# A two-layer decoder trunk: order of the out-projection's rows, lags of the norm feeds, and order of the key copies

## The chip, the cores and the metric

One core of one Trainium2 chip. The metric is device time in microseconds (us) of one execution; lower is better. Engines are named as the profile names them: PE (TensorE matmul) and PEld (its weight load), DVE (VectorE), ACT (ScalarE), POOL (GpSimd), SP (SyncE, which issues most DMAs here). L12 is line 12 of the kernel.

## The reference

x is 256 tokens by 1024. Two layers, each with a half-step SwiGLU FFN, a mixer, and a second half-step FFN:

```python
for layer in range(DEPTH):
    if layer == N_A_LAYERS:
        k_pads, v_pads = _shared_kv(x, kv_norm, w_kv, k_gain)
    x = x + 0.5 * _swiglu(_rms(x, norm_gain[layer, 0]), ffn_w_in[layer, 0], ffn_w_out[layer, 0])
    h = _rms(x, norm_gain[layer, 1])
    if layer < N_A_LAYERS:
        x = x + _hgrn2(h, a_w_in[layer], ...)
    else:
        x = x + _dilated_attention(h, b_w_q[j], b_q_gain[j], b_w_o[j], k_pads, v_pads, rel_bias)
    x = x + 0.5 * _swiglu(_rms(x, norm_gain[layer, 2]), ffn_w_in[layer, 1], ffn_w_out[layer, 1])
```

`_swiglu(h, w_in, w_out)` is `(silu(gate) * up) @ w_out` with `gate, up = split(h @ w_in)` and an inner width of 2816. The first mixer is a gated linear recurrence (8 heads), the second an attention with 16 heads of 64 in three groups of windows and dilations (128, 1), (512, 4), (2048, 16), with RMS-normed queries and keys and a shared bias by distance. Both mixers end with an out-projection of 1024 by 1024.

## The kernel before

**Precision by halves.** Every float32 operand of a large product is split into two fp32r numbers, high and low: ScalarE makes the high one by a copy or a scaled copy, VectorE subtracts it from the source to get the low one. Each product is then three matmuls: high by high, high by low, low by high. For weights this is `load_part` (L233 ff.): one or two DMAs on SP into one of 4 `raw` buffers, the ACT cast `wh` (L241), the DVE subtraction `wl` (L242), six buffers each. A part is two weight rows (two blocks of 128 in the contracted dimension) by 512 columns.

**Two kinds of product.** `products` (L248 ff.) takes tokens as the stationary side: for each of two token tiles `t`, three matmuls of 512 columns per weight row (L256, L257, L258), and after the last row a `consume(t, ...)`. `linear_T` (L271 ff.) takes weights as the stationary side: per pair of accumulators and part a "turn" of four pairs of matmuls (L312 with 512 columns: both halves of all 256 tokens at once; L308 with 256). In the first use of a norm its turns are sorted so that the first four need only rows 0 to 3 of the input, that is the left half of x, and turns five to eight the right half.

**The norm is applied late.** x itself, times the gain, is fed to the product; the factor 1/rms per token is applied to the result. `Norm.feed(n, t)` (L360 ff.) does this for the column half `n` (0 left, 1 right) and token tile `t` of x: four PE transposes into a PSUM bank (L365), four ACT scaled copies (L217) and four DVE operations (L220). A norm can have several operand sets with different gains: the norm ahead of layer 1's first FFN has two, `xT` for the FFN and `xK` for the keys and values of the attention. Then `square` (L375 ff.) sums squares on ACT (L380); after the fourth of these `finish` makes the scale by two DVE operations and a POOL power (L393), and `spread` (L398 ff.) transposes the scale on PE (L402) into a row by token that ACT copies out (L408). The products' consumers that need the row wait in a list until it is there.

**Ticks.** The order of the program is written by hand with a list of deferred jobs. `products` calls `tick()` after each token tile (six matmuls with a part of two rows, three with one row), `linear_T` after each turn. `defer(lag, fn)` runs `fn` in the lag-th tick from then; a job that was deferred just ahead of a tick with lag 1 runs in that very tick. A scheduler in the compiler then sets the final order on each engine; an engine runs its own queue in order.

**Lags the change touches.** `FEED_LAG = 1` between an add into x and the feed of that piece (L439); `ROW_LAG = 2` between `finish` and `spread` (L396); `NORM_LAG = 6` between the scaling of normed queries or keys and their transposes (L969).

**Adds and feeds.** `add_to_x` (L431 ff.) adds a finished accumulator into x on DVE (L435 after an out-projection, L437 after an FFN) and defers the feed of the next norm. In the FFN's second product the left half of the columns is finished 132 matmuls ahead of the right half's end.

**Out-projection** (L445 ff.). Both halves' accumulators are open together. Parts of two rows: left 0-5, then right 0-5, then both last parts are loaded and their rows run by turns, in order left 6, right 6, left 7, right 7. So when the left half is done, one row of the right half (six matmuls) is left.

**Attention.** The keys and values are made in four quarters of four heads each (`Quarter`, L1016 ff.). For three quarters the blocks are: all keys of two groups; the third's keys and the first's values; the other values. The last quarter has its own: first block keys of all three groups for the first pair of heads and the keys of group 0 for the second pair; second block the rest of the keys and some values; then the scores of the first pair; then the last values. `normed` (L952 ff.) squares, sums and scales keys, then transposes them on PE (`tpn`, L974), and `put_keys` (L1062 ff.) copies them out: for group 0 with halves, as each head has to stand in both halves of the partitions, high in its own and low, and the other way; for each of two heads ACT copies the high part (L1070), DVE makes the low one (L1071), ACT copies both to the other half (L1072 from PSUM, L1073 from SBUF). The other groups take one ACT copy (L1065). `scores` (L1126 ff.) reads them (L1136, L1137, L1143), `transposed` transposes the probabilities (`tpp`, L1189) and ACT copies them out (L1190). All transposes, scores and small products share the four PSUM banks of `psm`.

## Time and profile before

| | us |
|---|---|
| median of 3 runs | 1183.0 (1181.94 to 1184.51) |
| profiled execution | 1182.2, its span 1180.4 |
| PE busy | 1163.2 |
| PEld busy | 971.5 |
| DVE busy | 775.5 |
| ACT busy | 706.7 |
| POOL busy | 223.0 |

The profile is of one execution. Busy time is the union of an engine's instructions; a matmul's end is modelled, and matmuls overlap in the pipeline. In a timeline a line has the start in us from the span's start, the duration, the engine, the line, the operation, what it writes and reads, the shape and the count; the idle time of the engine just before it and what ended that time stand in square brackets.

### The profile page before, as it was taken

The page shows a single profiled execution, that of the slowest core. Times are in us where ns is not written, and L with a number is a line of the kernel's source. Part 1 is how long each engine was busy: PE and PEld are TensorE (multiplying, and loading weights), DVE is VectorE, ACT ScalarE, POOL GpSimd, SP SyncE. Part 2 cuts the span into 40 slices and gives each one's busy share as a digit, 9 for nine tenths or more (in the row PEclk, how much of TensorE's full clock was granted, in tenths as well). Part 3 has the DMA queues.
Part 4 walks back from the last instruction along what each step waited for, and adds up shares of the span by engine and source line. Part 5 has one row for each costly group of instructions (what it writes and reads, how often), then busy time and mean ns, then how long its engine had stood idle before and what let it go on. Part 6 is the DMA issues. An engine that isn't in the chain of part 4 may idle for free.

```text
span 1180.4 us, 18859 instructions
## 1 busy us (share of the span) xinstructions
PE 1163.2 (99%) x6774; PEld 971.5 (82%) x6774; DVE 775.5 (66%) x1263; ACT 706.7 (60%) x1283; POOL 223.0 (19%) x240
## 2 busy tenths in 40 slices
PE   9999999999999999999999999999999999999998
PEld 6888888888878888878888887888877777888886
DVE  6666655898766676666666556866776766666652
ACT  6656544876556565556556446657668686665541
POOL 2232201310012322003322002221210200323200
PEclk9999999999999999999999999999999999999999
DMA  8565666554545665555665665565465544556571
GB/s 273 159 207 176 208 201 182 177 160 163 163 150 168 196 189 203 181 179 167 188 197 173 223 192 181 174 195 176 139 182 149 153 130 130 168 175 203 185 234 44
DMA packets 181713, 209.28 MB, mean 177 GB/s; under 512 B 15483, under 2 KB 139843, under 8 KB 181620
## 3 DMA queue, kind: packets, MB, share of 16 engines
q1 hardware_dynamic: 180928, 207.68, 56.4%
q8 instruction: 53, 0.87, 0.3%
q10 hardware_dynamic: 692, 0.40, 0.1%
q14 instruction: 40, 0.33, 0.1%
HBM read 205.89 MB, written 1.10 MB: 175 GB/s over the span
## 4 chain that ended last, share of the span: by engine, by line
PE 83%; DVE 7%; issue 6%; ACT 2%; POOL 1%; DMA 1%; ACTq 0%; SPq 0%; DVEq 0%; POOLq 0%
PE acc L312 28%; PE acc L308 14%; PE acc L256 13%; PE acc L258 13%; PE acc L257 13%; DVE wl L242 2%; DMA raw<-in_ffn_w_in_dram 1%; PE tpn L974 1%; PE ob L1214 1%; PE tpp L1189 1%; POOL rs L428 1%; ACT wh L241 0%; PE tp L365 0%; DVE xT L220 0%; DVE kd L709 0%
## 5 line engine op out<-in xcount | busy, mean ns | idle before, releaser
L242 DVE TENSOR_TENSOR wl<-raw,wh 128x1024 fp32r<-128x1024 f32 x384 | 482.9, 1280 | 163.3 <-ACT wh L241 161.8
L241 ACT CAST wh<-raw 128x1024 fp32r<-128x1024 f32 x384 | 394.7, 1051 | 179.2 <-PE acc L258 151.4
L312 PE MATMUL acc<-xT,wh 128*128 128x512 f32 x1184 | 409.1, 398 | 0.8 <-DVE u L328 0.8
L308 PE MATMUL acc<-xT,wl 128*128 128x256 f32 x1184 | 308.1, 281 | 0.0
L312 PEld LDWEIGHTS acc<-xT,wh 128*128 128x128 f32 x1184 | 212.3, 188 | 42.2 <-DVE u L328 1.1
L308 PEld LDWEIGHTS acc<-xT,wl 128*128 128x128 f32 x1184 | 223.6, 189 | 12.9
L258 PE MATMUL acc<-wh,hid 128*128 128x512 f32 x352 | 137.8, 391 | 0.0
L256 PE MATMUL acc<-wh,hid 128*128 128x512 f32 x352 | 137.8, 391 | 0.0
L257 PE MATMUL acc<-wl,hid 128*128 128x512 f32 x352 | 137.5, 391 | 0.0
L209 DVE TENSOR_TENSOR hid<-u,hid 128x256 fp32r<-128x256 f32 x88 | 37.5, 426 | 133.7 <-ACT hid L208 133.7
L477 POOL TENSOR_TENSOR g<-g,row 128x256 f32<-128x256 f32 x88 | 65.6, 746 | 294.3 <-DVE g L328 282.8
L312 PE MATMUL acc<-xK,wh 128*128 128x512 f32 x352 | 119.7, 395 | 0.0
L478 ACT ACTIVATE g<-g 128x256 f32<-128x256 f32 x88 | 36.8, 419 | 97.1 <-POOL g L477 97.1
L479 POOL TENSOR_TENSOR u<-u,g 128x256 f32<-128x256 f32 x88 | 84.6, 961 | 50.8 <-ACT g L478 48.9
L256 PE MATMUL acc<-wh,xK 128*128 128x512 f32 x224 | 92.8, 414 | 0.0
L428 POOL TENSOR_TENSOR rs<-var,mhalf 128x8 f32<-128x8 f32 (+1 forms) x32 | 49.3, 1542 | 226.5 <-DVE var L426 226.5
L308 PE MATMUL acc<-xK,wl 128*128 128x256 f32 x352 | 90.5, 277 | 0.0
L208 ACT CAST hid<-u 128x256 fp32r<-128x256 f32 x88 | 35.7, 406 | 90.9 <-POOL u L479 90.9
L258 PE MATMUL acc<-wh,xK 128*128 128x512 f32 x224 | 88.7, 396 | 0.4 <-DVE xK L209 0.4
L257 PE MATMUL acc<-wl,xK 128*128 128x512 f32 x224 | 88.2, 394 | 0.0
L256 PE MATMUL acc<-wh,xT 128*128 128x512 f32 x192 | 78.0, 406 | 0.0
L258 PEld LDWEIGHTS acc<-wh,hid 128*128 128x128 f32 x352 | 66.0, 188 | 14.3
(176 smaller groups left out, 1472.0 us busy)
## 6 DMA issues: line engine op xcount, KB each, us to landing
raw<-in_ffn_w_in_dram SPq DMA_DIRECT2D x352, 256.0 KB, 4.2
raw<-in_ffn_w_out_dram SPq DMA_DIRECT2D x88, 512.0 KB, 4.6
raw<-in_w_kv_dram SPq DMA_DIRECT2D x72, 256.0 KB, 4.2
raw<-in_a_w_in_dram SPq DMA_DIRECT2D x32, 512.0 KB, 4.0
raw<-in_b_w_q_dram SPq DMA_DIRECT2D x24, 512.0 KB, 3.8
raw<-in_w_kv_dram SPq DMA_DIRECT2D x48, 128.0 KB, 2.4
raw<-in_a_w_out_dram SPq DMA_DIRECT2D x8, 512.0 KB, 3.5
raw<-in_b_w_o_dram SPq DMA_DIRECT2D x8, 512.0 KB, 3.7
```

Source lines behind the costliest of these rows:

```text
L209: nc.vector.tensor_tensor(l, src, h.bitcast(F32), op=ALU.subtract)
L241: casts.append(nc.scalar.copy(wh[:, :nk, :], raw[:, :nk, :]))
L242: nc.vector.tensor_tensor(wl[:, :nk, :], raw[:, :nk, :], wh[:, :nk, :].bitcast(F32), op=ALU.subtract)
L256: nc.tensor.matmul(ps[t], xs.h[:, kk, tok], wh[:, at, :], start=kk == 0, stop=False)
L257: nc.tensor.matmul(ps[t], xs.h[:, kk, tok], wl[:, at, :], start=False, stop=False)
L258: nc.tensor.matmul(ps[t], xs.l[:, kk, tok], wh[:, at, :], start=False, stop=kk == nkt - 1)
L308: nc.tensor.matmul(acc[:, 0:S], wl[:, k, w], xs.h[:, kk, :], start=False, stop=False)
L312: nc.tensor.matmul(acc, wh[:, k, w], xs.hl[:, kk, :, :].rearrange("p a t -> p (a t)"), start=kk == 0, stop=kk == KD - 1,)
L428: nc.gpsimd.tensor_tensor(r[:, :n], v[:, :n], mhalf[:, :n], op=ALU.pow)
L477: nc.gpsimd.tensor_tensor(g, g, norm.by_token, op=ALU.mult)
L478: nc.scalar.activation(g, g, AF.Silu)
L479: nc.gpsimd.tensor_tensor(u, u, g, op=ALU.mult)
```

## The change

1. `ROW_LAG` goes from 2 to 3.
2. `FEED_LAG` is now by half: 1 for the left, 2 for the right, after out-projections and FFNs alike. The right half's second feed thus runs in the tick after the last product's, which is the first tick of what follows.
3. In `feed` only the first operand set is put at once; the others follow three ticks later (`SECOND_LAG`), behind the square. Only the norm with `xT` and `xK` has a second set.
4. The out-projection's rows: left 0-5, right 0-3, then single rows left 6, right 4, right 5, left 7, right 6, right 7. When the left half is done, two rows of the right half (twelve matmuls) are left. A part is loaded where its first row is needed.
5. The transposes of the last quarter's keys come three ticks after their scaling (`LAST_LAG`), not six; the second pair's group 0 keys of its first block are put two ticks after the first's (`PAIR_LAG`).
6. `put_keys` for group 0: ACT copies the high parts of both heads from PSUM, then DVE makes both low parts, then ACT copies the high parts to the other half from SBUF (before: from PSUM), and DVE copies the low parts there (before: ACT). The queries' put gets the same order by engine: two ACT operations, then two DVE operations.

```diff
--- before.py
+++ after.py
@@ -40,24 +40,27 @@
 BIAS_LEN = (512, 128, 128)
 BT = 768
 SCW = S + P
-ROW_LAG = 2
+ROW_LAG = 3
 LB_LAG = 20
 SC_BUFS = 4
 WARM = 8
 WARM_ON = 10
-FEED_LAG = 1
+FEED_LAG = (1, 2)
+SECOND_LAG = 3
 GATE_LAG = 3
 SQUARE_LAG = 1
 MOVE_LAG = 6
 SQ0 = 4
 SQ_STEP = 1
 NORM_LAG = 6
+LAST_LAG = 3
 SCALE_LAG = 3
 LEVEL_LAG = 5
 UNIT_LAG0 = 3
 UNIT_LAG = 2
 SCORE_LAG = 5
 VALUE_LAG = 2
+PAIR_LAG = 2
 BLK = 32
 QUADS = (2, 8)
 DIAG_LAG = 5
@@ -363,14 +366,20 @@
             for c in range(4):
                 at = (4 * n + c) * P
                 nc.tensor.transpose(tp[:, c * P : (c + 1) * P], self.x[:, t, at : at + P], ident)
-            for g, halves in self.sets:
+
+            def put(g, halves):
                 halves.put_scaled(
                     4 * n,
                     slice(t * P, (t + 1) * P),
                     tp.rearrange("p (c t) -> p c t", c=4),
                     g[:, 4 * n : 4 * n + 4],
                 )
+
+            put(*self.sets[0])
             defer(SQUARE_LAG, lambda: self.square(n, t))
+            for g, halves in self.sets[1:]:
+
+                defer(SECOND_LAG, lambda g=g, halves=halves: put(g, halves))
 
         def square(self, n, t):
             if self.fed == 0:
@@ -436,7 +445,7 @@
         else:
             nc.vector.scalar_tensor_tensor(to, ps, scale, to, op0=ALU.mult, op1=ALU.add)
         if norm is not None:
-            defer(FEED_LAG, lambda: norm.feed(n, t))
+            defer(FEED_LAG[n], lambda: norm.feed(n, t))
         return to
 
     def half_of(w, n):
@@ -452,13 +461,17 @@
         def done(n):
             return lambda t, acc: add_to_x(x, n, t, acc, norm)
 
+        parts = {}
+
+        row_by_row = [(0, KD - 2), (1, KD - 4), (1, KD - 3), (0, KD - 1), (1, KD - 2), (1, KD - 1)]
         for n in range(2):
-            for k in range(0, KD - NK, NK):
+            for k in range(0, min(kk for nn, kk in row_by_row if nn == n), NK):
                 products(xs, ps[n], k, NK, KD, *part(n, k), done(n))
-        last = [part(n, KD - NK) for n in range(2)]
-        for k in range(NK):
-            for n in range(2):
-                products(xs, ps[n], KD - NK + k, 1, KD, *last[n], done(n), off=k)
+        for n, k in row_by_row:
+            k0 = k // NK * NK
+            if (n, k0) not in parts:
+                parts[n, k0] = part(n, k0)
+            products(xs, ps[n], k, 1, KD, *parts[n, k0], done(n), off=k - k0)
 
 
     def ffn(x, layer, f, norm, following, part_first=None):
@@ -949,7 +962,7 @@
 
             return slice(64 * c, 64 * c + 64), slice(64 - 64 * c, 128 - 64 * c)
 
-        def normed(ps, nh, mean, then):
+        def normed(ps, nh, mean, then, lag=NORM_LAG):
 
             sq = tmp4.tile([P, 512], F32, tag="s5", name="sqh")
             nc.scalar.activation(sq[:, : nh * HD], ps, AF.Square)
@@ -966,7 +979,7 @@
                     rs[:, :nh].unsqueeze(2).broadcast_to([P, nh, HD]),
                     op=ALU.mult,
                 )
-                defer(NORM_LAG, transposed)
+                defer(lag, transposed)
 
             def transposed():
                 tp = bank("tpn")
@@ -989,13 +1002,16 @@
                             qT[:, g - 1, 4 * a : 4 * a + 4, tok], reverse(tp), AF.Copy, scale=qkT[:, g : g + 1]
                         )
                         return
+                    ways = []
                     for c in range(2):
                         own, other = places(c)
                         to = q0[:, 8 * a + c : 8 * a + 8 : 2, tok]
-                        src, gain = reverse(tp)[own], qkT[own, 0:1]
-                        nc.scalar.activation(to[own], src, AF.Copy, scale=gain)
+                        ways.append((to[own], to[other], reverse(tp)[own], qkT[own, 0:1]))
+                    for high, low, src, gain in ways:
+                        nc.scalar.activation(high, src, AF.Copy, scale=gain)
+                    for high, low, src, gain in ways:
                         nc.vector.scalar_tensor_tensor(
-                            to[other], src, gain, to[own].bitcast(F32), op0=ALU.mult, op1=ALU.subtract
+                            low, src, gain, high.bitcast(F32), op0=ALU.mult, op1=ALU.subtract
                         )
 
                 normed(ps, 8, norm.eps(t), put)
@@ -1045,11 +1061,16 @@
                         c += n
 
                     def put(tp):
-                        for g, p0, p1, c0 in keys:
-                            self.put_keys(t, g, p0, p1, tp[:, c0 : c0 + p1 - p0, :])
+                        for i, (g, p0, p1, c0) in enumerate(keys):
+                            args = (t, g, p0, p1, tp[:, c0 : c0 + p1 - p0, :])
+                            if i > 0 and g == 0:
+
+                                defer(PAIR_LAG, lambda args=args: self.put_keys(*args))
+                            else:
+                                self.put_keys(*args)
 
                     if keys:
-                        normed(ps[:, : nk * P], 2 * nk, norm2.eps(t), put)
+                        normed(ps[:, : nk * P], 2 * nk, norm2.eps(t), put, NORM_LAG if self.j < 3 else LAST_LAG)
 
                 cols = []
                 for kind, g0, g1, p0, p1 in pieces:
@@ -1064,13 +1085,19 @@
                 if g > 0:
                     nc.scalar.copy(self.kT[:, g - 1, p0:p1, tok], tp)
                     return
+
+                ways = []
                 for c in range(2):
-                    own, other = places(c)
                     h, l = (v[:, 2 * p0 + c : 2 * p1 : 2, tok] for v in (self.kh, self.kl))
+                    ways.append((*places(c), h, l))
+                for own, other, h, l in ways:
                     nc.scalar.copy(h[own], tp[own])
+                for own, other, h, l in ways:
                     nc.vector.tensor_tensor(l[own], tp[own], h[own].bitcast(F32), op=ALU.subtract)
-                    nc.scalar.copy(h[other], tp[own])
-                    nc.scalar.copy(l[other], l[own].bitcast(F32))
+                for own, other, h, l in ways:
+                    nc.scalar.copy(h[other], h[own].bitcast(F32))
+                for own, other, h, l in ways:
+                    nc.vector.tensor_copy(l[other], l[own].bitcast(F32))
 
             def put_values(self, t, g, c0, c1, ps):
                 r = norm2.rstd(t)
```

## The prediction

> **What bounds the kernel now.** I read the page first: its first part and the chain that ended last.
>
> ```profile
> PE 1163.2 (99%) x6774; PEld 971.5 (82%) x6774; DVE 775.5 (66%) x1263; ACT 706.7 (60%) x1283; POOL 223.0 (19%) x240
> ...
> PE 83%; DVE 7%; issue 6%; ACT 2%; POOL 1%; DMA 1%; ACTq 0%; SPq 0%; DVEq 0%; POOLq 0%
> ```
>
> TensorE is busy for 99% and carries 83% of the chain, and the change takes no matmul and no transpose away. So it can only win where PE stands still, 1180.4 - 1163.2 = 17.2 us in all. The table of waits, for PE alone, says for whom it stands still:
>
> ```profile
> PE tp L365 <- DVE res L435: 3.3, 2, 1.7
> PE rp L402 <- POOL rstd L393: 2.4, 3, 1.4
> PE sp L1136 <- ACT kh L1072: 1.7, 1, 1.7
> ```
>
> Columns: total us, times, longest. These three are the largest, and each is a place that the change touches: the feeds after the out-projections, the transposes of the row scales, the keys. I then read the timeline engine by engine around each.
>
> **Left half earlier, right feed later (out-projection).** PE, then VectorE, at the end of the first out-projection; the last line is PE at the second:
>
> ```profile
> 334.01 0.66 PE L365 MATMUL tp<-ident,res 128*128 128x128 f32 x4 [1.65 <-DVE res L435]
> ```
> ```profile
> 329.33 1.37 DVE L435 TENSOR_TENSOR res<-acc,res 128x512 f32<-128x512 f32 x2 [1.09 <-PE acc L258]
> 331.09 1.23 DVE L242 TENSOR_TENSOR wl<-raw,wh 128x1024 fp32r<-128x1024 f32 x1 [0.39 <-ACT wh L241]
> 332.24 1.12 DVE L220 SCALAR_TENSOR_TENSOR xT<-tp,gT,xT 128x128 fp32r<-128x128 f32 x4
> 333.27 0.68 DVE L435 TENSOR_TENSOR res<-acc,res 128x512 f32<-128x512 f32 x1
> 333.87 1.12 DVE L220 SCALAR_TENSOR_TENSOR xT<-tp,gT,xT 128x128 fp32r<-128x128 f32 x4
> ```
> ```profile
> 991.13 0.65 PE L365 MATMUL tp<-ident,res 128*128 128x128 f32 x4 [1.67 <-DVE res L435]
> ```
>
> PE's last product is done at 334.01 - 1.65 = 332.36. The wait is put down to the third add (333.27), but the FFN's first matmul could not start then either: it reads both token halves of the first weight row, so it needs the first of the four pieces of the second L220 group, 333.87 + 1.12/4 = 334.15. That whole chain starts with the adds of the left half at 329.33. At present the left half ends 9 matmuls before the end (3 of its own second token tile, 6 of the last row of the right half); in the new order 15 (two rows of the right half). Matmul starts stand 0.23 apart:
>
> ```profile
> 928.50 0.39 PE L257 MATMUL acc<-wl,xK 128*128 128x512 f32 x1
> 928.72 0.39 PE L258 MATMUL acc<-wh,xK 128*128 128x512 f32 x1
> 928.95 0.49 PE L1189 MATMUL tpp<-ident,sc 128*128 128x128 f32 x3
> ```
>
> 6 x 0.23 = 1.38 earlier, so the first FFN matmul can start at 334.15 - 1.38 = 332.77 against 332.36: 0.41 of the 1.65 stays, 1.24 goes. Upper end: all 1.65. Lower end: the last row of the FFN's first chunk gets its weight buffer later in the new order (released 18 matmuls before the end instead of 24), so one more 1.23 us subtraction of L242 can fall between the adds and the feeds; then 1.38 - 1.23 = 0.15 is left. I take 1.24, as in the row order that is there. Two out-projections: **2.5 us**. The right feed's own step, one tick later, is costed at nothing: its eight transposes per boundary are the same work, and the FFN's first turn (made from the left half only) covers it. What is late next is turn five, which needs the right half; see the last rival. Nothing moves on the DMA queue but the order in which two weight parts of the out-projection are asked for: same eight loads, same bytes, four buffers ahead.
>
> **Scale transposes later.** PE at the three places where it waits for them (first and second out-projection, then the FFN with two operands):
>
> ```profile
> 340.64 0.43 PE L402 MATMUL rp<-ident,rstd 128*128 128x128 f32 x2 [0.51 <-POOL rstd L393]
> ```
> ```profile
> 997.76 0.43 PE L402 MATMUL rp<-ident,rstd 128*128 128x128 f32 x2 [0.49 <-POOL rstd L393]
> ```
> ```profile
> 530.28 0.43 PE L402 MATMUL rp<-ident,rstd 128*128 128x128 f32 x2 [1.44 <-POOL rstd L393]
> ```
>
> The right feed's extra tick and the row lag's extra tick put these two turns later, behind five turns instead of three. A turn is four pairs of matmuls, and a pair takes 0.35:
>
> ```profile
> 341.26 0.40 PE L312 MATMUL acc<-xT,wh 128*128 128x512 f32 x1
> 341.50 0.28 PE L308 MATMUL acc<-xT,wl 128*128 128x256 f32 x1
> 341.61 0.39 PE L312 MATMUL acc<-xT,wh 128*128 128x512 f32 x1
> ```
>
> After the first out-projection the FFN's pairs run from 334.4 (the transposes at 334.01 issued) to 340.13; less 0.6 for four more transposes that is 14 pairs, and at five turns, 20 pairs, they come 6 x 0.35 = 2.1 later, more than the 0.5 missing: **1.0 us** gained for both. At the third place the FFN starts at
>
> ```profile
> 520.63 0.39 PE L312 MATMUL acc<-xT,wh 128*128 128x512 f32 x1
> ```
>
> and PE stops at 528.84: 8.2 less 1.3 for eight transposes is some 20 pairs, five turns already. The queue there did not follow the text, and the lag alone gives nothing. There the second operands are the lever. ScalarE, then GpSimd:
>
> ```profile
> 524.46 1.18 ACT L217 ACTIVATE xK<-tp,gT 128x128 fp32r<-128x128 f32 x4
> 525.46 0.71 ACT L380 ACTIVATE junk<-res 128x512 f32<-128x512 f32 x1
> ```
> ```profile
> 528.60 1.63 POOL L393 TENSOR_TENSOR rstd<-tot,mhalf 128x2 f32<-128x2 f32 x1 [64.18 <-DVE tot L389]
> ```
>
> The last square (525.46) stands behind one xK group of 1.18, and VectorE has two such groups ahead of the scale. With both three ticks later the square starts about 1.0 earlier and VectorE has 2 x 1.1 less in front, so the scale is ready 1 to 2 us sooner: all **1.44** goes (lower end 0.8 if a weight subtraction of 1.23 takes the place). The xK work itself then falls into turns four and five; it is next read in the attention.
>
> **Keys.** PE, then ScalarE, at the first scores of the last quarter:
>
> ```profile
> 943.90 0.38 PE L1136 MATMUL sp<-kh,q 128*128 128x256 f32 x1 [0.24 <-DVE kl L1071]
> ...
> 946.21 0.38 PE L1136 MATMUL sp<-kh,q 128*128 128x256 f32 x1 [1.73 <-ACT kh L1072]
> ```
> ```profile
> 944.95 1.04 ACT L241 CAST wh<-raw 128x1024 fp32r<-128x1024 f32 x1
> 945.90 0.26 ACT L1072 CAST kh<-tpn 64x128 fp32r<-64x128 f32 x1
> ```
>
> The last key copy stands behind a weight cast, at the end of a row of copies that goes ACT, DVE, ACT, ACT for each half. Two edits act on it. The transposes of the last quarter come three ticks earlier: 18 matmuls, at least 18 x 0.23 = 4.1 us, against 1.97 us of waiting. And the second ScalarE copy reads SBUF instead of PSUM, so it no longer waits for VectorE; the fourth copy goes to VectorE:
>
> ```profile
> L1071 DVE TENSOR_TENSOR kl<-tpn,kh 64x256 fp32r<-64x256 f32 x12 | 5.0, 417 | 2.8 <-ACT kh L1070 2.5
> ...
> L1073 ACT CAST kl<-kl 64x256 fp32r<-64x256 f32 x12 | 4.8, 404 | 0.1
> ```
>
> That moves 4.8 us (and the last quarter's half-sized copies) from ScalarE to VectorE; by the L1071 row, which reads PSUM and has two operands, it costs VectorE at most about 5.0, on an engine that is busy for 66%, and at the least nothing; none of it is on PE's path. Gain: 0.24 + 1.73 = **2.0 us**; bounds 0 (the copies stay behind the cast) and 2.0. Can the transposes go so early? The second token tile's input:
>
> ```profile
> 926.03 0.69 DVE L963 TENSOR_TENSOR sqh<-acc,rs 128x512 f32<-128x512 f32 x1 [1.46 <-POOL rs L428]
> ```
>
> It is ready at 926.72; the tick behind which the transposes then stand ends with the 928.72 matmul above. Margin 2.0 us.
>
> **The clock.** The view by windows of 4 us (busy of PE, PEld, DVE, ACT, POOL, then granted clock):
>
> ```profile
> 332.00:336.00 4.00, 2.35 (x15) 1.82 (x14) 4.00 (x12) 4.00 (x14) 0.00 (x0) 1.00 0.44 131
> 944.00:948.00 4.00, 2.27 (x23) 1.64 (x24) 1.80 (x3) 3.84 (x11) 0.00 (x0) 1.00 0.00 0
> 948.00:952.00 4.00, 4.00 (x13) 2.82 (x12) 3.74 (x11) 3.34 (x9) 0.00 (x0) 0.57 0.68 240
> ```
>
> After the key wait the granted clock falls to 0.57 for a window, which costs 4 x 0.43 = **1.7 us**. If the wait goes, I expect this to go; bounds 0 and 1.7, and I take 1.7, because it follows the wait at once and nothing else stands near it. The Trainium skill ("TensorE: Matmul & The Clock Gate", section "HAM oscillation — how this bites in real kernels") gives the rule that only PE gaps over about 3.4 us must be avoided. By that rule the 1.97 us gap is not the cause and the 1.7 would stay lost; the trace disagrees so far, since the clock fell right behind that gap, though not behind the 1.65 us gap in the 332 window.
>
> **Sum.** 2.5 + 1.0 + 1.4 + 2.0 + 1.7 = 8.6 us. The profiled execution took 1182.2 us (span 1180.4), the median of the runs is 1183.0, 0.8 above it, so the forecast is 1183.0 - 8.6 = **1174.4 us**.
>
> **The rivals.** (1) PSUM banks run short. The earlier transposes take two of the four shared banks, and the put of the second pair holds them two ticks longer, exactly where the previous quarter's probabilities hold theirs long:
>
> ```profile
> 931.43 0.83 ACT L1190 COPY pT<-tpp 128x384 f32<-128x384 f32 x2
> ```
>
> The bank of the probability transpose at 928.95 (row above) is freed only by this, and the next scores need two banks. A new wait of about 2.0 with the clock drop of 1.7 there costs 3.7: 1183.0 - 8.6 + 3.7 = 1178.1. For: four banks (`psm`), and two scores, two probability transposes and two key transposes within three ticks. Against: PE's queue has acc products that can stand ahead. If it happens twice, 1181.8, no measurable change.
>
> (2) The lags do not bind: the queue's place for the row transposes (20 pairs instead of 12) shows an order not taken from the text. Then 1.0 + 1.4 stay: 1176.8.
>
> (3) The clock falls anyway, as the skill's rule would have it; worked from the window row, 1.7 less gain: 1176.1.
>
> (4) Slower: the right feed comes too late for turn five, at all four places where a fed norm enters such a loop. First out-projection, VectorE's last feed group:
>
> ```profile
> 338.61 1.13 DVE L220 SCALAR_TENSOR_TENSOR xT<-tp,gT,xT 128x128 fp32r<-128x128 f32 x4 [0.79 <-ACT xT L217]
> ```
>
> Turn five starts at 341.61 (the 17th pair) and needs the first piece at 338.61 + 0.28 = 338.89: 2.7 slack. The change takes 1.24 + 0.5 of waiting out in front of turn five, and a tick's delay is 4 x 0.35 = 1.4 more: 2.7 - 1.74 - 1.4 = -0.4 if nothing in the feed moves up with the adds. It turns the sum only if the wait reaches about 1.4 and trips the clock each time: 4 x (1.4 + 1.7) = 12.4 against 8.6, 1186.8. Against it: the adds start 1.38 earlier, which restores the slack to about +1.0.
>
> **How the numbers follow.** Chances: forecast 0.50; rival 1 once 0.15, twice 0.10; rival 2 0.10; rival 3 0.07; rival 4 0.08. A measurement of this kernel tells about 0.2%, 2.4 us. Faster: 0.50 + 0.15 + 0.10 + 0.07 = 0.82; same 0.10; slower 0.08. Range: low 1171.5 (the 2 x 0.41 left over at the out-projections gone as well, and runs up to 1.1 below the median, as the lowest shown); high 1180.5, past rivals 1 to 3 and the lower ends of the out-projection terms (2 x 1.1 less).
>
> **What would show it.** Right: PE's table of waits has no res L435, rstd L393 or kh line above 0.5; the first FFN matmuls follow the out-projection's last within 0.5; clock 1.00 through 930 to 960; PE busy total unchanged within 3 us and the span's idle below 10. Wrong: an equal wait under another name (tpn for ACT or DVE, or acc for xT at the fifth turn), or a second half-clock window.

## The result, and the profile after

The changed kernel takes 1174.87 us (median of 4 runs, 1174.53 to 1175.15), the kernel before, run beside it, 1183.62 (4 runs, 1181.94 to 1184.51): a ratio of 0.9928 [0.9916, 0.9939], so 0.7% less. The forecast was 1174.4. The two profiled executions stand at 1174.81 (span 1173.0) and 1182.22 (span 1180.4): 7.4 us less.

The page of the changed kernel, busy times and the shares of the chain that ended last:

```profile
PE 1160.3 (99%) x6774; PEld 970.3 (83%) x6774; DVE 781.0 (67%) x1283; ACT 701.9 (60%) x1263; POOL 225.1 (19%) x240
...
PE 88%; DVE 7%; issue 1%; ACT 1%; POOL 1%; DMA 1%; SPq 0%; ACTq 0%; DVEq 0%; POOLq 0%
```

PE still has its 6774 matmuls, and the 20 copies that went from ACT to DVE show in the counts. PE stands still for 1173.0 - 1160.3 = 12.7 us, 4.5 less than before; the other 2.9 are busy time (1163.2 - 1160.3). That is a balance of parts of both signs; the slow clock, 1.7, is one of them (below). The table of waits, for PE (total us, times, longest):

```profile
PE ob L1241 <- ACT kT L1086: 1.7, 1, 1.7
...
PE acc L315 <- DVE xT L223: 0.5, 1, 0.5
PE acc L315 <- DVE xK L223: 0.5, 1, 0.5
```

The three lines that the prediction started from are gone. The out-projections' entries went from 1.65 and 1.67 to 0.5 each, the scale transposes from 0.51, 0.49 and 1.44 to nothing, the keys from 1.97 to nothing. One new line is now the largest: the value product (`ob`, L1241) waits 1.7 for a key copy that it does not read. New too are 0.7 and 0.4 for the first loads from memory at the very start; in the traces of all kernels here the wait for x there ranges from nothing to 1.5, so spans of single traces differ by about 1 us for that reason alone.

**The entry.** PE at the end of the first out-projection, then DVE:

```profile
331.46 0.39 PE L261 MATMUL acc<-wh,xK 128*128 128x512 f32 x1
...
332.37 0.50 PE L315 MATMUL acc<-xT,wh 128*128 128x512 f32 x1 [0.52 <-DVE xT L223]
```
```profile
327.46 0.69 DVE L444 TENSOR_TENSOR res<-acc,res 128x512 f32<-128x512 f32 x1 [2.45 <-PE acc L261]
328.07 1.22 DVE L245 TENSOR_TENSOR wl<-raw,wh 128x1024 fp32r<-128x1024 f32 x1
329.20 0.69 DVE L444 TENSOR_TENSOR res<-acc,res 128x512 f32<-128x512 f32 x1
329.80 1.22 DVE L245 TENSOR_TENSOR wl<-raw,wh 128x1024 fp32r<-128x1024 f32 x1
330.93 2.15 DVE L223 SCALAR_TENSOR_TENSOR xT<-tp,gT,xT 128x128 fp32r<-128x128 f32 x8
333.00 1.28 DVE L444 TENSOR_TENSOR res<-acc,res 128x512 f32<-128x512 f32 x2
```

The left half's first add starts 331.85 - 327.46 = 4.39 ahead of the end of the last product; before it was 332.36 - 329.33 = 3.03. It moved 1.36 forward (worked out: 1.38). The right half's adds (333.00) now come behind the feeds. Two weight subtractions, not one, stand between the first left add and the feeds.

**The scales.** POOL, then PE, behind the first out-projection:

```profile
335.77 0.70 POOL L402 TENSOR_TENSOR rstd<-tot,mhalf 128x2 f32<-128x2 f32 x1 [34.65 <-DVE tot L398]
```
```profile
340.32 0.38 PE L411 MATMUL rp<-ident,rstd 128*128 128x128 f32 x2
```

The scale is ready at 336.47, 3.9 us ahead of its transposes; before, it came 0.05 ahead of them, after PE had waited. Counted from the FFN's first matmul it is ready after 4.1 us (332.37 to 336.47); before, after 6.2 (334.42 to 340.59). On DVE the first operation of the scale now stands ahead of the right half's feed:

```profile
335.52 0.17 DVE L398 TENSOR_SCALAR tot<-tot 128x2 f32<-128x2 f32 x1
...
336.57 2.15 DVE L223 SCALAR_TENSOR_TENSOR xT<-tp,gT,xT 128x128 fp32r<-128x128 f32 x8
```

Before, it stood behind all of that feed, at 339.65.

**The new wait.** PE at the first value product of the third quarter, which falls among the copies of the last quarter's keys, ACT beside it, and the windows of 4 us (busy of PE, PEld, DVE, ACT, POOL, then the granted clock, DMA share, GB/s):

```profile
928.94 0.46 PE L1170 MATMUL sp<-kT,qT 64*64 64x64 f32 x16
...
931.08 0.65 PE L1241 MATMUL ob<-pT,vt 128*64 128x256 f32 x4 [1.68 <-ACT kT L1086]
```
```profile
930.63 0.43 ACT L1086 COPY kT<-tpn 128x128 f32<-128x128 f32 x2
```
```profile
928.00:932.00 4.00, 2.32 (x43) 1.91 (x43) 3.02 (x12) 3.82 (x16) 0.00 (x0) 1.00 0.33 121
932.00:936.00 4.00, 4.00 (x29) 3.00 (x26) 2.48 (x14) 3.85 (x11) 1.01 (x1) 1.00 0.09 17
```

The value product reads probabilities and values of its own quarter, not keys. The copy that ended its wait emptied a bank of the four in `psm`, so I read this as a wait for the bank (see the experiments on the bank). The granted clock stays at 1.00 behind this wait; before, it fell to 0.57 behind the keys' 1.97.

**The start.** PE in the first FFN, where the wait for `u` was 0.8 before:

```profile
22.60 0.50 PE L315 MATMUL acc<-xT,wh 128*128 128x512 f32 x1 [0.29 <-DVE u L331]
```

Added up from the two traces: entries 1.13 + 1.17, scales 1.0 + 1.44, keys 1.97, clock 1.7, start 0.5, less 1.7 for the bank: 7.2. That this is close to the 7.4 between the spans is chance, because the list leaves out parts of both signs. If one follows PE matmul by matmul, the changed kernel is 9.0 us ahead in the last FFN's first product (the same matmul starts at 996.94 and, before, at 1005.90). Of the 1.8 beyond the list, 1.0 lies in the second value products of the first two quarters: their 24 matmuls stand in another order and take 1.48 instead of 2.01 and 1.96 (for the first, 853.77 to 855.25, and before 857.79 to 859.80). The other 0.8 is not broken down. Then 1.5 is lost again: 601 matmuls of the last FFN's first product, the same in the same order, take 105.7 in the changed kernel (996.94 to 1102.68) and took only 104.2 before (1005.90 to 1110.14). The edits do not touch these matmuls, and every trace but that of the kernel before is as slow there as the changed kernel's; more on this in the last section.

### The profile page after: what moved, and what is told of

It is laid out like the page before. It is cut to its first block, busy times and chain, and to the rows that moved or that the text cites. A ratio compares the mean times of both kernels' runs of the same rounds, so it can differ in the third digit from the quotient of the medians.

```text
span 1173.0 us, 18848 instructions
## 1 busy us (share of the span) xinstructions
PE 1160.3 (99%) x6774; PEld 970.3 (83%) x6774; DVE 781.0 (67%) x1283; ACT 701.9 (60%) x1263; POOL 225.1 (19%) x240
## 4 chain that ended last, share of the span: by engine, by line
PE 88%; DVE 7%; issue 1%; ACT 1%; POOL 1%; DMA 1%; SPq 0%; ACTq 0%; DVEq 0%; POOLq 0%
PE acc L315 29%; PE acc L311 15%; PE acc L259 13%; PE acc L261 13%; PE acc L260 13%; DVE wl L245 2%; PE ob L1241 1%; PE tpn L987 1%; POOL rs L437 1%; PE tpp L1216 1%; PE tp L368 1%; PE sp L1170 0%; DMA x<-in_x_dram 0%; DVE kd L722 0%; ACT wh L244 0%
## 5 line engine op out<-in xcount | busy, mean ns | idle before, releaser
L245 DVE TENSOR_TENSOR wl<-raw,wh 128x1024 fp32r<-128x1024 f32 x384 | 482.2, 1280 | 155.7 <-ACT wh L244 154.5
```

The costliest lines, as they stand in the source:

```text
L245: nc.vector.tensor_tensor(wl[:, :nk, :], raw[:, :nk, :], wh[:, :nk, :].bitcast(F32), op=ALU.subtract)
```

## The experiments

Each expectation sets a theory A against a rival or a theory B. All kernels start from the changed one, but for `f3_keys_only`, and were timed beside the kernel before. The changed kernel was not timed beside them (its own ratio is 0.9928), so others are set against it by ratio, or by the one trace of each. The last column is the mean granted clock of the single runs.

| kernel | median us | before | ratio | clock of its runs |
|---|---|---|---|---|
| e1_last6 | 1176.67 | 1183.59 | 0.9941 [0.9927, 0.9954] | 0.999; four at 0.998 |
| e2_oldkeys | 1178.3 | 1183.59 | 0.9956 [0.9943, 0.997] | 1.0; four at 0.996-0.998 |
| e3_oldrows | 1177.15 | 1183.59 | 0.9947 [0.9935, 0.996] | 0.999-1.0 |
| e5_rowlag2 | 1176.08 | 1183.59 | 0.9939 [0.9927, 0.9952] | 0.999-1.0 |
| e4_second_at_once | 1176.44 | 1183.76 | 0.9931 [0.9917, 0.9945] | 0.999-1.0 |
| e6_feed1 | 1175.07 | 1183.76 | 0.992 [0.9906, 0.9934] | 0.999-1.0 |
| e7_pair0 | 1174.33 | 1183.76 | 0.9915 [0.9901, 0.9929] | 0.999-1.0 |
| e8_last4 | 1176.03 | 1183.76 | 0.9925 [0.991, 0.9939] | three at 0.999-1.0; three at 0.997 |
| f1_rows3 | 1173.97 | 1182.12 | 0.9927 [0.9915, 0.9938] | 0.999-1.0 |
| f2_value3 | 1179.47 | 1182.12 | 0.9974 [0.9965, 0.9982] | two at 0.999; nine at 0.997-0.998 |
| f3_keys_only | 1180.13 | 1182.12 | 0.9982 [0.9973, 0.9991] | 0.999-1.0 |
| g1_both | 1174.11 | 1182.63 | 0.9927 [0.9914, 0.9941] | 0.999-1.0 |

Line numbers are those of the changed kernel, but two to three lower in `e2_oldkeys`, `e4_second_at_once` and `f3_keys_only`.

### The rows: `e3_oldrows`, `f1_rows3`

`e3_oldrows` goes back to the old order of the rows:

```diff
-        row_by_row = [(0, KD - 2), (1, KD - 4), (1, KD - 3), (0, KD - 1), (1, KD - 2), (1, KD - 1)]
+        row_by_row = [(0, KD - 2), (1, KD - 2), (0, KD - 1), (1, KD - 1)]
```

> The changed kernel with the old row order of the out-projection (left half one row ahead of the end, not two). Theory A (the earlier adds shorten the wait): PE's idle time at the two entries goes from 0.5 us back to about 1.6 each: 1177.1 us. Rival (the later right feed did it, as it no longer stands in front of the first FFN matmul): idle time stays at 0.5 and the time at 1174.9 us.

The waits of PE, and POOL:

```profile
PE tp L368 <- DVE res L444: 3.3, 2, 1.7
```
```profile
339.71 0.70 POOL L402 TENSOR_TENSOR rstd<-tot,mhalf 128x2 f32<-128x2 f32 x1 [38.33 <-DVE tot L398]
```

The entries are back as they were before, 3.3 against 1.0, so 2.3 us belong to the rows. The second line says more: the scale is ready at 340.41. The FFN's first matmul starts at 334.25 here, so that is after 6.2 us again, as before the change, and not after 4.1, with both lags still in place. So it is the order of the rows that makes the scale early. Its transposes do not wait here, because they stand behind 20 pairs (at 341.81).

`f1_rows3` goes the other way: the left half ends three rows ahead.

```diff
+        row_by_row = [(0, KD - 2), (1, KD - 4), (0, KD - 1), (1, KD - 3), (1, KD - 2), (1, KD - 1)]
```

> The changed kernel with the left half of the out-projection ending three rows ahead of the end (left 6, right 4, left 7, right 5, 6, 7), 18 matmuls instead of 12. Theory A (the chain from the left adds to the first FFN matmul ends the wait, and it moves with the adds): another 1.4 us of room takes away the 0.5 us that is left at each of the two entries: 1173.9 us. Rival (the weight subtractions on VectorE fill whatever room there is, as two of them already stand between the adds and the feeds): 0.5 us or more stays, 1174.9 us or above.

PE at the end of the first out-projection, and at its scale transposes, then DVE:

```profile
331.03 0.39 PE L261 MATMUL acc<-wh,xK 128*128 128x512 f32 x1
331.25 0.39 PE L315 MATMUL acc<-xT,wh 128*128 128x512 f32 x1
...
339.78 0.32 PE L411 MATMUL rp<-ident,rstd 128*128 128x128 f32 x1 [0.52 <-POOL rstd L402]
```
```profile
334.60 2.16 DVE L223 SCALAR_TENSOR_TENSOR xT<-tp,gT,xT 128x128 fp32r<-128x128 f32 x8
...
338.79 0.16 DVE L398 TENSOR_SCALAR tot<-tot 128x2 f32<-128x2 f32 x1
```

The first entry's wait is gone altogether (at the second, 0.1 of idle time is left). But the scale is now ready only at 339.73, 8.5 us behind the FFN's first matmul, and its transposes wait 0.52: the right half's feed stands ahead of the scale on DVE again. So the rows act on the scale through the order that the scheduler gives these operations, and a still earlier left half does not make the scale earlier still. Why it chose these orders, no run shows. The ratio equals the changed kernel's: what was won at the entries was in good part given back at the scale, nine microseconds later.

### The lags: `e5_rowlag2`, `e6_feed1`, `e4_second_at_once`

```diff
-ROW_LAG = 3
+ROW_LAG = 2
```

> The changed kernel with the row lag back at 2, so that the scale's transposes stand behind four turns instead of five. By the prediction's step (the lag buys the room): waits for rstd of some 0.1 to 0.9 us come back at three or four places: 1176 to 1177.3 us. Rival (the scale itself is ready earlier, as in the trace of the changed kernel it is ready 3.9 us ahead of its transposes, against 0.05 late before): four turns are still enough, no wait for rstd, 1174.9 us.

No scale transpose waits, though they stand behind 16 pairs instead of 20. The trace is 1.0 us longer than the changed kernel's (span 1174.0), and PE in the first FFN shows where:

```profile
26.44 0.50 PE L315 MATMUL acc<-xT,wh 128*128 128x512 f32 x1 [1.27 <-DVE u L331]
```

1.27 against 0.29. The other two traces with the old lag have 0.77 (the kernel before) and 1.18 (`f3_keys_only`) there, and no other trace with the new lag has a wait there. So the row lag's gain is at the start of the kernel, in the one FFN whose norm is not fed by an out-projection or an FFN before it, and not at the scale transposes.

```diff
-FEED_LAG = (1, 2)
+FEED_LAG = (1, 1)
```

> The changed kernel with the right half's feed back at one tick. In its order the scale's transposes then stand behind four turns, and the first left squares stand behind the feed copies again. Theory A (the later right feed lets the squares go first, and this is why the scale is ready 3 to 4 us earlier): the scale is ready about when it was before the change, some 6.3 us after the first FFN matmul, which four turns (16 x 0.35 = 5.6 us and the transposes) just meet: waits for rstd of 0 to 0.5 us at each out-projection, and about 1 us at the FFN with two operands is not expected, as the second operands are still late: 1174.9 to 1176 us. Rival (the prediction's: the right feed costs and brings nothing by itself): 1174.9 us with the scale ready as early as now.

No wait appears; the scale is ready at 336.28. The right half's later feed brings nothing by itself, and costs nothing.

`e4_second_at_once` puts both operand sets in `feed` again:

```diff
-            put(*self.sets[0])
+            for g, halves in self.sets:
+                put(g, halves)
             ...
```

> The changed kernel with both operand sets fed at once. Theory A (the second operands held up the square, so the scale): the scale of the two-operand norm is ready 2 to 3 us later and PE waits for it 0.5 to 1.5 us: 1175.5 to 1176.4 us. Rival (the right feed's tick and the row lag's are enough room): no wait, 1174.9 us.

PE and POOL ahead of the FFN with two operands, and DVE beside POOL:

```profile
527.34 0.43 PE L409 MATMUL rp<-ident,rstd 128*128 128x128 f32 x2 [1.36 <-POOL rstd L400]
```
```profile
525.65 1.63 POOL L400 TENSOR_TENSOR rstd<-tot,mhalf 128x2 f32<-128x2 f32 x1 [63.54 <-DVE tot L396]
```
```profile
525.48 1.22 DVE L245 TENSOR_TENSOR wl<-raw,wh 128x1024 fp32r<-128x1024 f32 x1
```

The wait is back with its old size (1.44 before), and the median is 1.37 above that of `e6_feed1`, which was timed beside it. Counted from the FFN's first matmul, the scale is ready after 9.6 us (517.68 to 527.28) against 6.2 in `e6_feed1` (518.13 to 524.33): 2.5 later because its sums stand behind the second set's work, and 0.93 because the POOL power took 1.63 instead of 0.70 (see the last section).

### The keys: `e1_last6`, `e2_oldkeys`, `f3_keys_only`

Two edits act on the keys. Each of the first two kernels undoes one.

```diff
-LAST_LAG = 3
+LAST_LAG = 6
```

> The changed kernel with the last quarter's key transposes back at six ticks; the order of the key copies by engine stays. Theory A (the earlier transposes took the key wait away): a wait of 1 to 2 us for kh or kl comes back at the first scores of the last quarter, with up to 1.7 us of half clock, and the new 1.7 us wait of the value product for kT goes, as the banks are as before: 1174 to 1177 us. Theory B (the new order of the copies alone took it away): no key wait, no kT wait, 1173.0 us, 1.9 below the changed kernel.

There is no wait for `kh` or `kl`: the order by engine alone removes it. But PE waits just after, and the clock falls. PE, ACT, windows:

```profile
950.96 0.44 PE L987 MATMUL tpn<-ident,sqh 128*128 128x128 f32 x2 [2.10 <-ACT kT L1086]
```
```profile
948.99 1.48 ACT L1110 ACTIVATE vn<-acc,rstd 64x128 f32<-64x128 f32 x4
950.47 0.43 ACT L1086 COPY kT<-tpn 128x128 f32<-128x128 f32 x2
```
```profile
948.00:952.00 4.00, 1.90 (x26) 1.50 (x25) 1.99 (x3) 3.88 (x13) 0.00 (x0) 0.95 0.47 147
952.00:956.00 4.00, 4.00 (x14) 3.09 (x14) 2.03 (x10) 3.93 (x11) 0.00 (x0) 0.62 0.05 18
```

A key transpose waits 2.10 for a bank that ACT empties late, since four value copies of 1.48 stand ahead of the key copies. The mechanism that I expected to fail here, the copies' order, held; the time was lost at a place that neither theory had named.

`e2_oldkeys` keeps `LAST_LAG` at 3 and takes the old row of copies, head by head:

```diff
-                for own, other, h, l in ways:
                     nc.vector.tensor_tensor(l[own], tp[own], h[own].bitcast(F32), op=ALU.subtract)
-                for own, other, h, l in ways:
-                    nc.scalar.copy(h[other], h[own].bitcast(F32))
-                for own, other, h, l in ways:
-                    nc.vector.tensor_copy(l[other], l[own].bitcast(F32))
+                    nc.scalar.copy(h[other], tp[own])
+                    nc.scalar.copy(l[other], l[own].bitcast(F32))
```

> The changed kernel with the old order of the key copies (ACT, DVE, ACT, ACT for each head, low copy on ScalarE); the transposes stay three ticks early. Theory A (the three ticks do it): no wait of the scores for keys, since 4 us of earlier start cover 2 us of waiting; the banks are held longer by the back and forth, so the value product's wait of 1.7 us grows by 0.5 to 1.5: 1175.4 to 1176.5 us. Theory B (the order does it): the scores wait 1 to 2 us for kh again, perhaps with 1.7 us of half clock: 1176 to 1178.6 us.

PE, windows:

```profile
934.41 0.58 PE L1238 MATMUL ob<-pT,vt 128*64 128x256 f32 x2 [2.76 <-DVE negm L1187]
```
```profile
932.00:936.00 4.00, 1.59 (x20) 1.38 (x22) 2.94 (x14) 3.85 (x13) 0.35 (x1) 0.82 0.01 4
```

Again no wait for the keys' halves, so the three ticks alone remove it too; again a longer one for a bank in its place, 2.76, and the clock falls behind it. One more thing comes back: the second value products of the first two quarters take 2.00 and 1.98, as in the kernel before (2.01 and 1.96), while they take 1.48 in every trace with the new order of copies. So that order is worth a further 1.0 us at a place that was not priced.

`f3_keys_only` is the kernel before with edits 5 and 6 alone (row order, lags and operand sets as they were; only the last weight parts of the out-projections are loaded where they are first needed, as in the changed kernel).

> The kernel before with the two edits of the keys alone (transposes three ticks early with the second pair two ticks late; copies in order by engine); rows, feeds, second operands and row lag as before. Theory A (the key wait cost 2.0 us and the half clock behind it 1.7; the new bank wait takes 1.7 back and leaves the clock alone): 2.0 below the kernel before, 1181.7 us, and no window of half clock in the trace. Rival (the clock falls for another reason, or behind the new wait too): half clock shows again and the time is within 0.5 us of the kernel before.

1180.13 against 1182.12: 2.0 less, as worked out from 2.0 for the wait and 1.7 for the clock, less 1.7 for the bank. The hit is in part luck, for the sum lacks the 1.0 of the value products, and the runs of this kernel spread by 4.5. Waits of PE, then windows:

```profile
PE tp L368 <- DVE res L442: 3.3, 2, 1.7
PE rp L409 <- POOL rstd L400: 2.4, 3, 1.4
PE ob L1239 <- ACT kT L1084: 1.7, 1, 1.7
```
```profile
932.00:936.00 4.00, 2.32 (x28) 1.75 (x29) 2.84 (x12) 3.79 (x15) 0.00 (x0) 1.00 0.01 3
936.00:940.00 4.00, 4.00 (x22) 3.29 (x21) 3.26 (x15) 3.91 (x11) 1.01 (x1) 1.00 0.20 45
```

The other parts' waits stand as in the kernel before, the bank wait is the changed kernel's, and the clock stays at 1.00.

### The bank: `e7_pair0`, `e8_last4`, `f2_value3`, `g1_both`

`e7_pair0` puts the second pair's keys at once, so that their bank comes free earlier:

```diff
-                            if i > 0 and g == 0:
+                            if False:
```

> The changed kernel with the second pair's keys put at once, not two ticks later. Theory A (the two ticks hold the PSUM banks, and the value product's 1.7 us wait comes from that): the key copies for kT come up to 1 us earlier and the wait falls to 0.5 to 1.0: 1174 us. Theory B (the early transposes alone make the banks short, whatever the second pair does): the wait stays at 1.7 or grows, 1175 us.

Waits of PE:

```profile
PE tpp L1216 <- DVE kl L1096: 0.7, 1, 0.7
PE ob L1241 <- DVE kl L1096: 0.7, 1, 0.7
```

1.4 in two pieces instead of 1.7 in one, and what ends them is now the keys' low part, the last reader of that bank. So which copy holds the bank decides whom the wait falls on; its sum hardly changes.

```diff
-LAST_LAG = 3
+LAST_LAG = 4
```

> The changed kernel with the last quarter's key transposes at four ticks, not three. Theory A (what decides is where the transposes fall among the users of the four banks): at four ticks the second transpose and the value product meet otherwise, and a wait of 0 to 1 us is left in place of 1.7: 1173 to 1174.2 us. Theory B (any early transpose costs the bank wait): 1.7 to 2.5 us of waiting, 1175 to 1177 us, the upper end if the clock falls to half behind it.

PE, windows:

```profile
932.68 0.69 PE L1241 MATMUL ob<-pT,vt 128*64 128x256 f32 x2 [2.35 <-DVE var L435]
```
```profile
932.00:936.00 4.00, 3.32 (x28) 2.34 (x28) 3.23 (x16) 3.83 (x14) 1.01 (x1) 0.59 0.44 145
```

One tick later for the keys, and the wait is longer, 2.35, and the clock falls behind it. The row names a variance that empties no bank; just ahead of it on DVE, at 932.45, stands the end of the reading of a score bank (L1190).

`f2_value3` has `VALUE_LAG = 3` beside the edit of `e7_pair0`, so that the value products ask for their bank a tick later.

> The changed kernel with the second pair's keys put at once and the value product one tick later (in all quarters). Theory A (the value product waits for a PSUM bank that the early key transposes hold): one tick, 6 matmuls or 1.4 us, covers the 0.7 us of waiting that is left at it without the pair's lag; only the 0.7 us of the probability transpose behind it may stay: 1173 to 1174 us. Rival (the bank wait moves on to the next user of the banks, now the probability transposes): the same 1.4 us in all, 1174.3 us or more.

The value product waits 2.6, a score 0.8 more, and the clock falls: the rival's way, and more than it foresaw. Windows:

```profile
936.00:940.00 4.00, 4.00 (x27) 2.79 (x25) 3.75 (x15) 3.94 (x11) 2.01 (x2) 0.60 0.46 148
```

`g1_both` joins `f1_rows3` and `e7_pair0`.

> The changed kernel with both alterations that took waits away by themselves: the left half of the out-projection three rows ahead of the end, and the second pair's keys put at once. If they are independent: the bank wait of 1.7 falls to about 1.4 in two pieces, as without the pair's lag alone, and the entry waits of 0.5 each to 0 and 0.3, with the 0.5 wait for the first out-projection's scale: about 1.0 us below the changed kernel, a ratio of 0.992 or a little less to the kernel before. Rival (a changed order upstream moves the waits elsewhere): a ratio of 0.993 or more.

Its trace has a span of 1171.8, 1.2 below the changed kernel's, its ratio, 0.9927, is the same. No version tried is separably faster than the changed kernel. No tried edit removed the bank wait; a fifth bank for `psm` was not tried, so that the lack of banks causes it is argued from the traces and not shown by an edit: the waiting instruction never reads what ended its wait, and the releaser changes with whoever has just emptied a bank.

## Why the prediction was right

**The bound.** Right: no work of PE's went away, and the gain is what PE no longer stands still, plus the clock. The line on idle time missed: 12.7 and not below 10, since the bank wait (1.7), the two half microseconds at the entries and 1.1 for the first loads stand in it. The bank wait is also nearly what the prediction had named as a sign of being wrong, an equal wait under another name; it took back 1.7 of what the keys had gained. The range's low end does not follow from its own terms: 1174.4 - 0.8 - 1.1 is 1172.5, not 1171.5. The result is far from either.

**Rows, 2 x 1.24.** Right: 1.13 and 1.17 in the traces, 2.3 by `e3_oldrows`. The lower bound's second subtraction did come, but the chain from the first left add to the piece that PE needs kept its length (327.46 to 330.93 + 5 x 0.27 = 332.28 is 4.82; it was 334.15 - 329.33 = 4.82), since the subtraction filled time in which DVE had stood idle.

**Scale transposes, 1.0.** The size was right, the step is one of two. The prediction credited the lag, "6 x 0.35 = 2.1 later, more than the 0.5 missing". The queue did go from 14 to 20 pairs, and that suffices: in `e3_oldrows`, where the scale is as late as before, nothing waits. But the new order of the rows also makes the scale 2.1 us earlier, counted from the FFN's first matmul, and then nothing waits with the old lag either (`e5_rowlag2`). What the lag itself earns, 0.5 to 1.0 at the kernel's start, the prediction did not see.

**Right feed, nothing.** Right (`e6_feed1`). Rival 4's late turn five did not happen: no `acc` wait is above 0.5.

**Second operands, 1.44.** Right in size and place: 1.36 and 1.37 (`e4_second_at_once`). "1 to 2 us sooner" was too little: counted from the FFN's first matmul it is 3.4, of which 0.93 is the POOL power's own time.

**Keys, 2.0.** Right; but the two edits were taken to share the gain, and either suffices (`e1_last6`, `e2_oldkeys`). What both together buy is a shorter bank wait, 1.7, where one alone has 2.10 or 2.76. The order of the copies earns another 1.0 in the value products (`e2_oldkeys`), which the prediction did not see.

**Clock, 1.7.** Right in the traces: no window below 1.00 at the keys in the changed kernel, nor in `f3_keys_only`. Across runs it is less. Of the 52 runs of the kernel before that stood beside the experiments, 32 have a mean granted clock of 0.998 or less, 20 of 0.999 or more, and their mean times differ by 0.9 (1183.4 and 1182.5), so the profiled execution's 1.7 is not lost in each run. Even the 0.9 is not firm: taken apart by the four groups that were timed together, the difference is 1.2, -0.9, 2.5 and 0.1. The Trainium skill's rule ("TensorE: Matmul & The Clock Gate", section "HAM oscillation — how this bites in real kernels"), that gaps above some 3.4 us are to be avoided, would have had neither 1.97 nor 2.10 matter; the traces disagree.

**What the sum left out.** Rival 1's mechanism came true, once, where it was named, at 1.7 for its 2.0, but without the drop of the clock. Against that, the value products gave 1.0, the start 0.5 and smaller places 0.8 that were not priced. So the profiled pair is 9.0 apart up to the last FFN, for 8.6 forecast: the total is right because unpriced losses and gains nearly cancel, which is luck. The spans are only 7.4 apart, because the profiled execution of the kernel before ran its last FFN 1.5 faster than the other traces do. The median beside the changed kernel (1183.62) was 0.6 above that of the prediction. The runs of the kernel before spread by 1.9 to 4.7 us among those timed together, those of the changed kernel by 0.6 (4 runs). The clock explains a part of that; `f3_keys_only`, with no run below 0.999, still spreads by 4.5. The two paces of an FFN (last section) are a candidate for the rest, but no run shows that they make the spread.

## What to carry to other kernels

Where PE is busy for 99%, price a reordering by the waits of PE one at a time, and ask of each edit what it makes ready earlier as well as what it puts later: two edits can each remove the same wait, and then neither alone is its cause. Where the waiting instruction does not read what its releaser made, look for a buffer that it waits for; here, moving one user of a rotating pool mostly moved that wait to another user. Before adding up waits from two traces, check that the stretches in which nothing was changed take equally long. Take the longest single wait as seriously as the sum: here 1.7 cost 1.7, while 2.1 cost nearly twice that.

## What the runs showed of the hardware

**The clock fell behind waits of 2.1 us and more, and behind 0.24 and 1.73 together, not behind single ones of 1.7.** Single PE waits of 1.65 to 1.70 (the kernel before's entries, the changed kernel, `e3_oldrows`, `f3_keys_only`) were never followed by a half-clock stretch in a trace. Waits of 0.24 and 1.73 a moment apart (the kernel before), and of 2.10, 2.35, 2.6 and 2.76, were followed by some 3.4 us at half clock in each trace. Whether it happens seems to differ from run to run: going by the mean granted clock, the kernels with such a wait have runs of both kinds, and those at 0.999 or more are faster by 2.0 (`e1_last6`), 2.2 (`e2_oldkeys`), 1.2 (`e8_last4`) and 1.6 (`f2_value3`), of 1 against 4, 1 against 4, 3 against 3 and 2 against 9 runs.

**A power of 128 x 2 on POOL takes 0.70, or 1.63 beside a subtraction on DVE.** In the kernel before (528.60), `f3_keys_only` (527.13), `e4_second_at_once` (525.65), `f1_rows3` (987.64) and `g1_both` (987.00) it took 1.60 to 1.63, and each time a weight subtraction (L245, L242 in the kernel before; both inputs in SBUF) had started 0.16 to 0.18 earlier; POOL ended 0.55 to 0.58 after the subtraction did. In all six norms of the changed kernel it took 0.69 or 0.70. The Trainium skill has the rule for it ("SBUF — State Buffer", section "Who interferes with whom"): an instruction of DVE with two SBUF inputs contends with one of GpSimd that reads SBUF, and the order of issue decides who blocks. The traces agree where DVE came first. Where POOL came first, DVE lost nothing that shows, in `f1_rows3`, POOL and then DVE:

```profile
339.03 0.70 POOL L402 TENSOR_TENSOR rstd<-tot,mhalf 128x2 f32<-128x2 f32 x1 [38.39 <-DVE tot L398]
```
```profile
339.09 1.23 DVE L245 TENSOR_TENSOR wl<-raw,wh 128x1024 fp32r<-128x1024 f32 x1
```

No run put the two apart on purpose, so the contention is read from these rows, not shown by an edit. It was 0.93 of the 1.44 that the second operands were credited with.

**The same matmuls ran at two paces.** An FFN's first product repeats a matmul of 512 and one of 256 columns. These windows of 80 us lie wholly inside such products: two of the kernel before, two of `f3_keys_only`, one of the changed kernel (columns as above):

```profile
560.00:640.00 80.00, 80.00 (x456) 69.48 (x455) 53.14 (x71) 47.20 (x85) 24.16 (x30) 1.00 0.60 188
1020.00:1100.00 80.00, 80.00 (x463) 69.89 (x462) 52.21 (x73) 46.91 (x87) 23.61 (x29) 1.00 0.61 189
```
```profile
360.00:440.00 80.00, 80.00 (x463) 69.90 (x463) 52.82 (x74) 46.19 (x85) 24.05 (x29) 1.00 0.63 191
1016.00:1096.00 80.00, 80.00 (x456) 69.59 (x456) 53.13 (x73) 47.88 (x87) 23.69 (x29) 1.00 0.61 190
```
```profile
1012.00:1092.00 80.00, 80.00 (x457) 69.45 (x456) 53.19 (x73) 47.50 (x86) 24.10 (x29) 1.00 0.60 189
```

PE is busy throughout and the clock is 1.00 in all five, yet it gets through 463 matmuls in two of them and 456 or 457 in the others. Over a whole product that makes the 1.5 us by which the last FFN of the kernel before was shorter. What sets the pace, no run shows; the changed kernel's trace has the slower one in all four FFNs.
